# Moving one weight split, two activations and one later split in the start-up of a short-convolution kernel

## The chip, the cores and the metric

The kernel runs on one core of a Trainium2 chip. The core has five engines that run their own instruction queues in order and meet only through semaphores: TensorE (PE, matrix products; PEld is its weight load), VectorE (DVE, element-wise work), ScalarE (ACT, activations and copies), GpSimd (POOL, element-wise work on SBUF) and SyncE (SP, which issues the DMA transfers). Matrix products are written to PSUM, which has eight banks of 128 x 512 fp32 here; everything else lies in SBUF or in DRAM. The metric is the device time of one execution in microseconds; lower is better. A comparison of this kernel can tell two versions apart when they differ by about 0.2% of the time.

## The reference, cut to what matters

The depth is one, so that only the gated short-convolution layer runs, on 1024 tokens of width 1024, with an inner width of 2048:

```python
def short_conv_mixer(u, w_in, conv_w, w_out):
    z, bg, cg, v = jnp.split(u @ w_in.astype(u.dtype), 4, axis=-1)
    y = bg * causal_dwconv(cg * v, conv_w) * jax.nn.silu(z)
    return y @ w_out.astype(u.dtype)

u = rms_norm(h, pre_norm[i])
m = short_conv_mixer(u, sc_w_in[j], sc_conv_w[j], sc_w_out[j])
h = h + rms_norm(m, post_norm[i])
```

## The kernel before, in words

The result has to have fp32 accuracy. Each fp32 operand is therefore split into an upper part (a rounded copy, made by ScalarE) and a lower part (operand minus copy, made by VectorE), and a product of two operands becomes three matmuls: lower by upper, upper by lower, upper by upper (lines 189 to 191). `split` (lines 139 to 141) does this for a weight; `split_w(p, part)` names the tiles `w`.

The first multiplication, by `w_in`, takes the 64 column blocks of 128 two at a time: 32 pairs, two for each of 16 chunks of the inner width. Pair 2c holds the columns `cg` and `v` of chunk c, pair 2c+1 holds `z` and `bg`. Each pair is a 2 x 2 block product done with seven products instead of eight (Strassen's scheme in Winograd's form). The products are called a, b, c, e, d, f, g and run in this order on TensorE; each has 12 matmuls of 128 x 128 by 128 x 512. Products a, c, d and g add up in one PSUM bank, x; e and f in a second, v; b has a third, y. Before a next product may add to a bank, what stands in it has to be read: `snap` copies the bank behind products a, c and e to a tile `sna`, `snc` or `sne` (ScalarE, line 197), and a VectorE addition reads the bank behind b, d and f (lines 213, 218, 223). So d waits for the copy behind c, f for the copy behind e, and g for the addition `sne` behind d.

The weights of a pair are needed in four parts. Part 0 and part 3 are splits of raw blocks: part 0 is A11 and A12 (products a and b), part 3 is A22 (product g). Parts 1 and 2 are splits of four sums S that GpSimd forms in `add_s` (lines 133 to 137): part 1 serves c and e, part 2 serves d and f. On the other side stand the blocks `u` of the normalised, transposed input: `u_a`, `u_b`, `u_e`, `u_f` are parts of it, and `u_c`, `u_d`, `u_g` are split from differences T (lines 537 to 543, `t_sub`); `u_g` comes from -T4, which the second `t_sub` call writes. All `u` stay in SBUF through the whole first half.

The order on each engine is the program's order, written out by hand; no scheduler moves anything. Up to line 568 stands the head: pair 0 is multiplied in the plain way (no Strassen) while the input is normalised and transposed (`turn2`, `second`), with the products of pair 1 between, which end with c, e, d, f, g at lines 549 to 563. Behind the head comes a loop over the pairs 2 to 31; in pair 2 the function `first_chunk` adds to each product the work that completes chunk 0 (its convolution `cv`, two Silu activations, multiplications, and the store `y_d`). In each pair the loop also splits the weights of the next pair: part 0 behind b, part 1 behind e, part 2 behind f and part 3 behind g. `fetch` queues the load of a pair's raw weights on SP; three buffers, `raw`, take turns, and one of their turns is taken by the split `w1_1`.

The second half multiplies by `w_out` in the same manner from line 691 on.

In the text below, `w3_1` is part 3 of pair 1 (tile numbers of a profile row are left out there: it reads `w<-raw`), `w0_2` is part 0 of pair 2, and so on. An upper copy of a weight is the ACT row `L140`, a lower part the DVE row `L141`.

Of the kernel before, what the change touches and what calls it, by code (L numbers as in the profile page):

```python
# [8 lines left out]
F32 = mybir.dt.float32  # L9
# [9 lines left out]
def kernel(  # L19
# [16 lines left out]
    nc = tc.nc  # L36
# [32 lines left out]
    def flat(t):  # L69
        return t.rearrange("p a b -> p (a b)")  # L70
# [52 lines left out]
    def add_s(p, part):  # L123

        if p >= len(PAIRS):
            return
        r = raws[p]
        a11, a12, a21, a22 = (flat(r[:, n, k * KH : (k + 1) * KH]) for n in (0, 1) for k in (0, 1))
        if part == 0:
            sums[p] = raw.tile([P, 4, HB], F32, tag="sum", name=f"sum_{p}", bufs=1)  # L130
        s = sums[p]
        if part == 0:
            nc.gpsimd.tensor_add(s[:, 1], a21, a22)  # L133
            nc.gpsimd.tensor_sub(s[:, 0], s[:, 1], a11)
        else:
            nc.gpsimd.tensor_sub(s[:, 2], a11, a21)  # L136
            nc.gpsimd.tensor_sub(s[:, 3], a12, s[:, 0])  # L137

    def split(src, hi, lo):
        nc.scalar.copy(hi, src)  # L140
        nc.vector.tensor_sub(lo, src, hi.bitcast(F32))  # L141

    def split_w(p, part):

        if p >= len(PAIRS):
            return
        n = 2 * HB if part < 3 else HB
        tag = "w8" if part < 3 else "w4"
        if p == 1 and part == 1:
            t = raw.tile([P, 2, n], F32R, tag="raw", name=f"w{part}_{p}")  # L150
        else:
            t = wp.tile([P, 2, n], F32R, tag=tag, name=f"w{part}_{p}", bufs=3 if part < 3 else 2)
        if part == 0:
            src = flat(raws[p][:, 0])
        elif part == 3:
            src = flat(raws[p][:, 1, KH:])
        else:
            src = flat(sums[p][:, 2 * (part - 1) : 2 * part])
        split(src, t[:, 0], t[:, 1])
        wt[p, part] = t  # L160
# [4 lines left out]
    UH, UL = {}, {}  # L165
# [10 lines left out]
    def product(p, i, ks=None):  # L176

        part, off = WHERE[i]
        w = wt[p, part]
        which = {"b": "y", "e": "v", "f": "v"}.get(i, "x")  # L180
        first = i in "abe"
        if first and (p, which) not in banks:
            banks[p, which] = bank(f"p{which}_{p}")
        ps = banks[p, which]
        for k in range(KH) if ks is None else ks:
            hi = w[:, 0, off + k * P : off + (k + 1) * P]
            lo = w[:, 1, off + k * P : off + (k + 1) * P]
            last = k == KH - 1
            nc.tensor.matmul(ps, lo, UH[i][:, k], start=first and k == 0, stop=False, skip_group_check=True)  # L189
            nc.tensor.matmul(ps, hi, UL[i][:, k], start=False, stop=False, skip_group_check=True)  # L190
            nc.tensor.matmul(ps, hi, UH[i][:, k], start=False, stop=last, skip_group_check=True)  # L191
# [12 lines left out]
    def after(p, i):  # L204


        c = p // 2
        x_, v_ = banks[p, "x"], banks.get((p, "v"))
        if i in "ace":
            snap(p, i)  # L210
        if i == "b":
            t = sn[p, "a"]
            nc.vector.tensor_add(t, banks[p, "y"], t)
        elif i == "c" and p % 2:
            nc.scalar.activation(sn[p, "a"], sn[p, "a"], AF.Silu)
        elif i == "d":
            t = sn[p, "e"]
            nc.vector.tensor_add(t, x_, t)  # L218
            if p % 2:
                nc.gpsimd.tensor_mul(t, t, cvs[c][:, HB:])  # L220
        elif i == "f":
            t = sn[p, "c"]
            nc.vector.tensor_add(t, v_, t)  # L223
            if p % 2:
                nc.scalar.activation(t, t, AF.Silu)
                nc.gpsimd.tensor_mul(cvs[c][:, HB:], t, sn[p, "e"])
            else:
                nc.gpsimd.tensor_mul(gpad[:, TAPS - 1 + HB :], t, sn[p, "e"])  # L228
        elif i == "g":
            if p % 2:  # L230
                cv = cvs[c][:, :HB]
                nc.vector.tensor_mul(cv, x_, cv)
                nc.vector.tensor_mul(cv, cv, sn[p, "a"])
                y_done(c, cvs.pop(c))
            else:
                nc.vector.tensor_mul(gpad[:, TAPS - 1 : TAPS - 1 + HB], x_, sn[p, "a"])
                conv(c)
# [4 lines left out]
    def y_done(c, cv):  # L242
        nc.sync.dma_start(y_d[:, c], cv)
        done[c] = cv
# [48 lines left out]
    bt = flat(xa).rearrange("p (q k l) -> p q k l", q=2, k=KH)  # L293
# [193 lines left out]
    def plain_late(kk, part):  # L487

        for n in (0, 1):
            plain(0, n, 1, part, [kk], first=part == 1 and kk == 0, last=part == 0 and kk == KH - 1)  # L490
# [12 lines left out]
    turn2(2)  # L503
    second(2)
    nc.vector.tensor_add(sn[1, "a"], banks[1, "x"], sn[1, "a"])
    split_w(1, 3)
    plain_late(0, 0)
    plain_late(1, 1)
    turn2(3)
# [11 lines left out]
    def halves(a, j):  # L521
        return a[:, 2 * j : 2 * j + 2].rearrange("p k (t l) -> p k t l", t=TH)

    def t_halves(i, src):
        hi, lo = ((lambda j, u=u: halves(u[i], j)) for u in (UH, UL))
        return (
            lambda j: nc.scalar.copy(hi(j), src(j)),
            lambda j: nc.vector.tensor_sub(lo(j), src(j), hi(j).bitcast(F32)),
        )

    def t_split(i, src):
        hi, lo = t_halves(i, src)
        for j in range(2):
            hi(j)
            lo(j)

    def t_sub(q):
        for j in range(2):
# [14 lines left out]
    product(1, "e")  # L553
    snap(1, "e")
    product(1, "d")
    g_hi, g_lo = t_halves("g", lambda j: halves(bt[:, 1], j))
    g_hi(0)
    g_lo(0)
    g_hi(1)
    nc.vector.tensor_add(sn[1, "e"], banks[1, "x"], sn[1, "e"])  # L560
    g_lo(1)
    product(1, "f")
    product(1, "g")
    split_w(2, 0)
# [12 lines left out]
    def conv(c):  # L577
        cv = tmp.tile([P, L], F32, tag="cv", name=f"cv_{c}", bufs=2)
        nc.scalar.activation(cv, gpad[:, :L], AF.Copy, scale=tap(c, 0))  # L579
        for j in range(1, TAPS):  # L580
            nc.vector.scalar_tensor_tensor(  # L581
                cv, gpad[:, j : j + L], tap(c, j), cv, op0=ALU.mult, op1=ALU.add
            )
        cvs[c] = cv

    def first_chunk(i):

        if i == "":
            g = gpad[:, TAPS - 1 : TAPS - 1 + HB]
            nc.scalar.copy(g, banks[0, 0, 0])  # L590
            nc.vector.tensor_mul(g, banks[0, 1, 0], g)
            nc.vector.tensor_mul(gpad[:, TAPS - 1 + HB :], sn[0, 0], sn[0, 1])
            split_w(2, 1)
            conv(0)
            nc.gpsimd.tensor_mul(cvs[0][:, HB:], cvs[0][:, HB:], sn[1, "e"])
        elif i == "a":
            split_w(2, 2)
        elif i == "b":
            cv = cvs[0]
            nc.scalar.activation(sn[1, "c"], sn[1, "c"], AF.Silu)  # L600
            nc.scalar.activation(sn[1, "a"], sn[1, "a"], AF.Silu)
            nc.gpsimd.tensor_mul(cv[:, HB:], cv[:, HB:], sn[1, "c"])
            split_w(2, 3)
        elif i == "c":
            cv = cvs.pop(0)
            nc.vector.tensor_mul(cv[:, :HB], banks[1, "x"], cv[:, :HB])
            nc.vector.tensor_mul(cv[:, :HB], sn[1, "a"], cv[:, :HB])
            y_done(0, cv)
# [40 lines left out]
    for p in range(2, len(PAIRS)):  # L649
        q, prev = p + 1, p // 2 - 1  # L650
        for i in ORDER:
            product(p, i)
            after(p, i)
            if p == 2:
                first_chunk(i)
            if i == "a" and p < END:
                add_s(q, 0)
                if p in TODO:
                    fetch_t(TODO[p])
                if p % 2 == 0 and p > 2:  # L660
                    fetch_s(prev)
                if p + 2 <= END:
                    fetch(p + 2)
            if p == END - 1 and i in "cd":
                fetch_unit()
            if p == END:
                if i in "abcdg":
                    split_unit()
                    fetch_unit()
            elif i == "b":  # L670
                split_w(q, 0)
                add_s(q, 1)
                if p in TODO:
                    add_t(TODO[p], nc.gpsimd if p % 2 else nc.vector)
                if p == 3 or p % 2 == 0 and p > 2:
                    add_y(prev)
            elif i == "e":
                split_w(q, 1)
            elif i == "f":
                split_w(q, 2)  # L680
            elif i == "g":
                split_w(q, 3)
# [149 lines left out]
```

## Time and profile before

| What | Value |
|---|---|
| median of 3 runs | 795.43 us (795.42 to 795.58) |
| the profiled execution's own time | 795.87 us |
| its span, first to last instruction | 794.1 us |
| PE busy | 783.7 us (99% of the span), 3502 matmuls |
| DVE busy | 531.8 us (67%) |
| ACT busy | 308.7 us (39%) |
| POOL busy | 290.9 us (37%) |
| DMA | 114.38 MB, mean 144 GB/s |

A row of the timeline gives the start and the length in microseconds, the engine, the line, the operation and its tiles, and in brackets how long the engine had been idle and what ended this. The end of a matmul is modelled, so that neighbouring matmuls overlap in the rows: how fast they follow each other is read from their starts. Several equal instructions in a row are shown as one with a count.

### The profile page before, as it was taken

What the parts mean: (1) busy time and instruction counts of PE and PEld (TensorE: products, weight loads), DVE (VectorE), ACT (ScalarE), POOL (GpSimd) and SP (SyncE); (2) the same over time, 40 slices, a digit from 0 to 9 for tenths busy, and PEclk for the clock granted to TensorE, in tenths of its full rate; (3) what the DMA queues carried; (4) which work ended last, traced back from release to release, by engine and by line L of the source; (5) the groups of instructions that cost most, each with busy time, mean ns of one, the idle gap of its engine ahead of it and who ended that gap; (6) DMA issues with size and microseconds to landing.
All of it is one profiled execution on the core that took longest, in us unless ns stands there. A gap on an engine that the chain in (4) does not pass through costs nothing.

```text
span 794.1 us, 9047 instructions
## 1 busy us (share of the span) xinstructions
PE 783.7 (99%) x3502; PEld 648.9 (82%) x3502; DVE 531.8 (67%) x578; ACT 308.7 (39%) x424; POOL 290.9 (37%) x196
## 2 busy tenths in 40 slices
PE   8999999999999999999999999999999999999996
PEld 7877888888888888888888888888888888888885
DVE  5799676767676767676666666666666857633766
ACT  7555333342433333333333332323333637544441
POOL 1608634443444444447444444444344100000020
PEclk9999999999999999999999999999999999999998
DMA  9130351516170706165433324141515669455237
GB/s 321 53 106 6 89 198 54 199 53 211 42 245 8 252 25 227 44 209 174 130 96 103 114 86 145 54 146 53 163 38 178 233 215 418 181 205 212 106 109 262
DMA packets 94282, 114.38 MB, mean 144 GB/s; under 512 B 2920, under 2 KB 68512, under 8 KB 92192
## 3 DMA queue, kind: packets, MB, share of 16 engines
q1 hardware_dynamic: 94224, 113.81, 42.1%
q8 instruction: 27, 0.44, 0.2%
q14 instruction: 15, 0.12, 0.0%
q10 hardware_dynamic: 16, 0.00, 0.0%
HBM read 84.44 MB, written 29.36 MB: 143 GB/s over the span
## 4 chain that ended last, share of the span: by engine, by line
PE 90%; issue 4%; POOL 3%; DMA 1%; DVE 1%; ACT 0%; SPq 0%; DVEq 0%; POOLq 0%
PE px L189 13%; PE px L190 13%; PE px L191 13%; PE pv L189 7%; PE pv L190 7%; PE pv L191 7%; PE po_x L711 4%; PE po_x L712 4%; PE po_x L710 4%; PE py L189 3%; PE py L191 3%; PE py L190 3%; PE po_v L711 2%; PE po_v L712 2%; PE po_v L710 2%
## 5 line engine op out<-in xcount | busy, mean ns | idle before, releaser
L141 DVE TENSOR_TENSOR w<-sum,w 128x1024 fp32r<-128x1024 f32 x62 | 92.6, 1493 | 80.9 <-ACT w L140 80.9
L141 DVE TENSOR_TENSOR w<-raw,w 128x1024 fp32r<-128x1024 f32 (+1 forms) x62 | 98.3, 1587 | 6.0 <-ACT w L140 6.0
L140 ACT CAST w<-sum 128x1024 fp32r<-128x1024 f32 x62 | 65.0, 1049 | 65.7 <-issue 54.5
L581 DVE SCALAR_TENSOR_TENSOR cv<-gpad,cw,cv 128x1024 f32<-128x1024 f32 x32 | 64.4, 2012 | 19.7 <-ACT cv L579 19.1
L140 ACT CAST w<-raw 128x1024 fp32r<-128x1024 f32 (+1 forms) x62 | 51.5, 833 | 60.3 <-PE py L191 58.7
L228 POOL TENSOR_TENSOR gpad<-snc,sne 128x512 f32<-128x512 f32 x15 | 19.4, 1296 | 138.9 <-DVE snc L223 138.9
L136 POOL TENSOR_TENSOR sum<-raw 128x512 f32<-128x512 f32 x31 | 61.6, 1986 | 0.0
L220 POOL TENSOR_TENSOR sne<-sne,cv 128x512 f32<-128x512 f32 x15 | 20.5, 1367 | 102.1 <-DVE sne L218 86.9
L223 DVE TENSOR_TENSOR snc<-pv,snc 128x512 f32<-128x512 f32 x30 | 20.7, 691 | 52.4 <-PE pv L191 52.4
L750 POOL TENSOR_TENSOR acc<-acc,xr 128x512 f32<-128x512 f32 x4 | 6.9, 1722 | 133.3 <-DVE acc L749 133.3
L137 POOL TENSOR_TENSOR sum<-raw,sum 128x512 f32<-128x512 f32 x31 | 55.2, 1780 | 0.0
L133 POOL TENSOR_TENSOR sum<-raw 128x512 f32<-128x512 f32 x31 | 41.5, 1338 | 32.5 <-DVE w L141 32.5
L189 PE MATMUL px<-u_g,w 128*128 128x512 f32 x124 | 48.4, 391 | 1.4 <-DVE sne L218 0.7
L189 PE MATMUL px<-u_d,w 128*128 128x512 f32 x124 | 48.4, 390 | 0.3 <-ACT snc L197 0.3
L189 PE MATMUL py<-u_b,w 128*128 128x512 f32 x124 | 48.4, 391 | 0.0
L189 PE MATMUL px<-u_a,w 128*128 128x512 f32 x124 | 48.3, 390 | 0.0
L190 PE MATMUL px<-u_d,w 128*128 128x512 f32 x124 | 48.3, 389 | 0.0
L190 PE MATMUL px<-u_g,w 128*128 128x512 f32 x124 | 48.3, 389 | 0.0
L191 PE MATMUL py<-u_b,w 128*128 128x512 f32 x124 | 48.3, 389 | 0.0
L191 PE MATMUL px<-u_a,w 128*128 128x512 f32 x124 | 48.2, 389 | 0.0
L190 PE MATMUL py<-u_b,w 128*128 128x512 f32 x124 | 48.2, 389 | 0.0
L190 PE MATMUL px<-u_a,w 128*128 128x512 f32 x124 | 48.2, 389 | 0.0
(253 smaller groups left out, 2071.8 us busy)
## 6 DMA issues: line engine op xcount, KB each, us to landing
raw<-in_sc_w_in SPq DMA_DIRECT2D x64, 512.0 KB, 5.3
y_d<-cv SPq DMA_DIRECT2D x16, 512.0 KB, 3.2
t<-in_sc_w_out SPq DMA_DIRECT2D x8, 1024.0 KB, 6.0
t_d<-t SPq DMA_DIRECT2D x8, 1024.0 KB, 4.3
s_d<-s SPq DMA_DIRECT2D x8, 768.0 KB, 3.3
s<-y_d SPq DMA_DIRECT2D x8, 512.0 KB, 4.5
xr<-in_x SPq DMA_DIRECT2D x8, 512.0 KB, 4.6
out<-acc SPq DMA_DIRECT2D x12, 256.0 KB, 2.5
```

The costliest lines, as they stand in the source:

```text
L133: nc.gpsimd.tensor_add(s[:, 1], a21, a22)
L136: nc.gpsimd.tensor_sub(s[:, 2], a11, a21)
L137: nc.gpsimd.tensor_sub(s[:, 3], a12, s[:, 0])
L140: nc.scalar.copy(hi, src)
L141: nc.vector.tensor_sub(lo, src, hi.bitcast(F32))
L189: nc.tensor.matmul(ps, lo, UH[i][:, k], start=first and k == 0, stop=False, skip_group_check=True)
L190: nc.tensor.matmul(ps, hi, UL[i][:, k], start=False, stop=False, skip_group_check=True)
L191: nc.tensor.matmul(ps, hi, UH[i][:, k], start=False, stop=last, skip_group_check=True)
L581: nc.vector.scalar_tensor_tensor(cv, gpad[:, j : j + L], tap(c, j), cv, op0=ALU.mult, op1=ALU.add)
L710: nc.tensor.matmul(ps, lo, u[:, 0, k], start=first, stop=False, skip_group_check=True)
L711: nc.tensor.matmul(ps, hi, u[:, 1, k], start=False, stop=False, skip_group_check=True)
L712: nc.tensor.matmul(ps, hi, u[:, 0, k], start=False, stop=last, skip_group_check=True)
```

## The change

Three things move. No arithmetic is added or taken away.

- The split `w3_1` (A22 of pair 1) stood in the head between the third and the fourth block of `turn2` and `second`. It now stands behind product d of pair 1. The addition `sne` follows it, and both halves of the split of `u_g` follow that; before, the addition stood between the lower parts of the two halves. A helper that let the halves be taken apart is gone with it.
- In pair 2 the two Silu activations of chunk 0 and the GpSimd multiplication that uses one of them stood behind product b; they now stand behind product c. The multiplications of the first half of chunk 0 and its store stood behind c and now stand behind d.
- The split of part 1 of pair 3, in pair 2, stood behind product e and now stands behind product d. In all later pairs it stays behind e.

```diff
     nc.vector.tensor_add(sn[1, "a"], banks[1, "x"], sn[1, "a"])
-    split_w(1, 3)
     plain_late(0, 0)
...
     def t_split(i, src):
-        hi, lo = t_halves(i, src)
         for j in range(2):
-            hi(j)
-            lo(j)
+            hi, lo = (halves(u[i], j) for u in (UH, UL))
+            split(src(j), hi, lo)
...
     product(1, "d")
-    g_hi, g_lo = t_halves("g", lambda j: halves(bt[:, 1], j))
-    g_hi(0)
-    g_lo(0)
-    g_hi(1)
+    split_w(1, 3)
     nc.vector.tensor_add(sn[1, "e"], banks[1, "x"], sn[1, "e"])
-    g_lo(1)
+    t_split("g", lambda j: halves(bt[:, 1], j))
     product(1, "f")
...
         elif i == "b":
+            split_w(2, 3)
+        elif i == "c":
             cv = cvs[0]
             nc.scalar.activation(sn[1, "c"], sn[1, "c"], AF.Silu)
             nc.scalar.activation(sn[1, "a"], sn[1, "a"], AF.Silu)
             nc.gpsimd.tensor_mul(cv[:, HB:], cv[:, HB:], sn[1, "c"])
-            split_w(2, 3)
-        elif i == "c":
+        elif i == "d":
             cv = cvs.pop(0)
             nc.vector.tensor_mul(cv[:, :HB], banks[1, "x"], cv[:, :HB])
...
-            elif i == "e":
+            elif i == ("e" if p > 2 else "d"):
                 split_w(q, 1)
```

More of the change, by code (lines that the diff above doesn't have):

```diff
@@ L522, in halves @@
         return a[:, 2 * j : 2 * j + 2].rearrange("p k (t l) -> p k t l", t=TH)
[L524 to L529, printed above, removed]
     def t_split(i, src):
-        hi, lo = t_halves(i, src)
         for j in range(2):
-            hi(j)
-            lo(j)
+            hi, lo = (halves(u[i], j) for u in (UH, UL))
+            split(src(j), hi, lo)
     def t_sub(q):
```

## The prediction

> **What bounds the kernel now.** I read the page's busy times first, then TensorE's view of waits, then its timeline around each wait, then the timelines of the engines that ended them.
>
> ```profile
> PE 783.7 (99%) x3502; PEld 648.9 (82%) x3502; DVE 531.8 (67%) x578; ACT 308.7 (39%) x424; POOL 290.9 (37%) x196
> ```
>
> TensorE is busy for 783.7 of 794.1 us. Another engine can matter only where TensorE stands still. Three of its waits lie in the stretch that the change touches:
>
> ```profile
> PE px L189 <- DVE sne L218: 0.7, 1, 0.7
> ...
> PE px L189 <- ACT w L140: 0.6, 1, 0.6
> ...
> PE px L189 <- ACT snc L197: 0.3, 1, 0.3
> ```
>
> In TensorE's timeline these are the starts of products g of pair 1, d of pair 2 and g of pair 2. The rows are the last matmul ahead of the first stop, the stopped ones, and the first matmuls of the products that serve as marks (12 matmuls each):
>
> ```profile
> 58.37 0.39 PE L191 MATMUL pv<-u_f,w 128*128 128x512 f32 x1
> 59.40 0.47 PE L189 MATMUL px<-u_g,w 128*128 128x512 f32 x1 [0.64 <-ACT w L140]
> 62.22 0.39 PE L189 MATMUL px<-u_a,w 128*128 128x512 f32 x1
> ...
> 70.38 0.39 PE L189 MATMUL pv<-u_e,w 128*128 128x512 f32 x1
> ...
> 73.55 0.50 PE L189 MATMUL px<-u_d,w 128*128 128x512 f32 x1 [0.29 <-ACT snc L197]
> ...
> 76.45 0.39 PE L189 MATMUL pv<-u_f,w 128*128 128x512 f32 x1
> ...
> 80.05 0.50 PE L189 MATMUL px<-u_g,w 128*128 128x512 f32 x1 [0.72 <-DVE sne L218]
> ...
> 82.90 0.39 PE L189 MATMUL px<-u_a,w 128*128 128x512 f32 x1
> ```
>
> From 62.22 to 70.38 three products (a, b, c) pass without a stop: 8.16 us, 2.72 each, 0.227 per matmul. With that pace each stop is priced by starts, which also takes in the slow first matmul behind it (0.47 to 0.50 long):
>
> - g of pair 1: it could start at 58.37 + 0.227 = 58.60 and a at 61.32; a starts at 62.22. Lost: 0.90.
> - d of pair 2: from e at 70.38, f could start at 75.82; it starts at 76.45. Lost: 0.63.
> - g of pair 2: from f at 76.45, a of pair 3 could start at 81.89; it starts at 82.90. Lost: 1.01.
>
> Together 2.54 us. TensorE's view of waits names none behind 82.90, so time gained here stays gained unless a new stop arises.
>
> **The change, part by part.**
>
> *First part: w3_1 and sne.* VectorE in the head:
>
> ```profile
> 40.95 1.17 DVE L141 TENSOR_TENSOR w<-raw,w 128x512 fp32r<-128x512 f32 x1
> 42.04 0.74 DVE L480 SCALAR_TENSOR_TENSOR xb<-pk,gcol,xa 128x512 f32<-128x512 f32 x1
> ...
> 53.90 2.35 DVE L543 TENSOR_TENSOR xa<-xa,xb 128x1024 f32<-128x1024 f32 x2
> 57.43 1.23 DVE L528 TENSOR_TENSOR u_g<-xa,u_g 128x1024 fp32r<-128x1024 f32 x1 [1.18 <-ACT u_g L527]
> 58.57 0.68 DVE L560 TENSOR_TENSOR sne<-px,sne 128x512 f32<-128x512 f32 x1
> 59.17 1.21 DVE L528 TENSOR_TENSOR u_g<-xa,u_g 128x1024 fp32r<-128x1024 f32 x1
> 60.30 1.22 DVE L141 TENSOR_TENSOR w<-raw,w 128x1024 fp32r<-128x1024 f32 x1
> ```
>
> Product g (59.40) starts just behind the end of the addition `sne` (58.57 + 0.68 = 59.25), although the page's row names the copy of another weight. The addition stood behind the first lower half of `u_g`, and that behind a gap of 1.18. Product d had ended long before: its last matmul is 12 places ahead of 58.37, at 55.65, and 0.39 long, so at 56.04. ScalarE in the same stretch, and the transposes that the earlier VectorE row has to wait for:
>
> ```profile
> 40.03 1.03 PE L347 MATMUL pk<-ident,xb 128*128 128x128 f32 x8
> ```
> ```profile
> 53.35 0.59 ACT L197 COPY sne<-pv 128x512 f32<-128x512 f32 x1 [1.21 <-PE pv L191]
> 56.34 2.01 ACT L527 CAST u_g<-xa 128x1024 fp32r<-128x1024 f32 x2 [2.40 <-DVE xa L543]
> 58.24 1.04 ACT L140 CAST w<-raw 128x1024 fp32r<-128x1024 f32 x1
> ```
>
> Taking w3_1's lower part out frees 42.04 - 40.95 = 1.09 us of VectorE. The next row needs the transposes, which end at 41.06, so VectorE runs 0.98 ahead from there, and `t_sub` ends at 55.27 instead of 56.25. Its upper part goes into ScalarE's 2.40 gap ahead of `u_g`, and costs nothing there. Its lower part comes behind `t_sub`: 0.68 to 1.17 us. The 1.17 is the row above, taken while GpSimd worked; the 0.68 is the 128x512 addition. I take 0.68, since GpSimd has nothing to do at that place before the head is over: 55.95. Then `sne`, not before 56.04: done by 56.8. The new wait of VectorE on d therefore costs some 0.1; behind it stand both halves of `u_g` and w0_2. First half of `u_g`: its copy (56.34 - 0.98 = 55.36, about 1.0 long) is there at 56.4, so it ends at 58.0; the second at 59.2; w0_2's lower part at 60.4. TensorE asks for them at 58.83 (second matmul of g), 60.19 (its eighth) and 61.32 (a). Slack 0.8, 1.0 and 0.9: the stop goes, **-0.90**. With no head start at all and with 1.17, `sne` ends at 58.1, the first half at 59.3, and g is held 0.5: the gain is then 0.4.
>
> The load of pair 3 now takes the buffer of `w1_1`, free when e ends (53.32), and not that of w3_1's block at 42.1; pair 4's takes the latter, behind 55.95. Both stand on SP's queue with nothing urgent between.
>
> ```profile
> raw<-in_sc_w_in SPq DMA_DIRECT2D x4, 512.0 KB, 5.0
> ```
>
> That is the DMA view of 30 to 70 us, the four loads of pairs 3 and 4: 5.0 us to landing, so pair 3 lies in SBUF near 59. It is first read at about 68 (below). Cost nothing.
>
> *What follows from it.* GpSimd's sums for pair 2 start when `u_g` is done (head memory):
>
> ```profile
> 60.50 2.17 POOL L133 TENSOR_TENSOR sum<-raw 128x512 f32<-128x512 f32 x1
> ...
> 65.71 2.29 POOL L137 TENSOR_TENSOR sum<-raw,sum 128x512 f32<-128x512 f32 x1
> ```
> ```profile
> 65.18 1.67 DVE L141 TENSOR_TENSOR w<-sum,w 128x1024 fp32r<-128x1024 f32 x1 [0.57 <-ACT w L140]
> 66.77 3.63 DVE L581 SCALAR_TENSOR_TENSOR cv<-gpad,cw,cv 128x1024 f32<-128x1024 f32 x2
> 70.32 1.22 DVE L141 TENSOR_TENSOR w<-sum,w 128x1024 fp32r<-128x1024 f32 x1
> ```
>
> They move up by 60.38 - 59.2 = about 1.2, TensorE by 0.90. So w1_2 is whole at 66.85 - 1.2 = 65.65 and c of pair 2 asks at 61.32 + 5.44 = 66.76; w2_2 is whole at 70.3, d asks at 72.20. No stop.
>
> *Second part: Silu behind c.* ScalarE in pair 2:
>
> ```profile
> 68.03 1.06 ACT L140 CAST w<-sum 128x1024 fp32r<-128x1024 f32 x1 [1.37 <-POOL sum L137]
> 69.11 1.28 ACT L600 ACT_TABLE_LOAD   x1
> ...
> 71.47 1.56 ACT L140 CAST w<-raw 128x512 fp32r<-128x512 f32 x2
> 72.92 0.58 ACT L197 COPY snc<-px 128x512 f32<-128x512 f32 x1
> 73.40 0.58 ACT L197 COPY sne<-pv 128x512 f32<-128x512 f32 x1
> ```
>
> Table load and both Silus take 71.47 - 69.11 = 2.36, and `snc` stands behind them though c was over long before. After: the casts of w2_2 (66.8 to 67.9), w3_2 and w0_3 (to 69.4), then `snc` at c's end, 69.48 + 0.17 (the modelled 0.39 beyond the 0.227 step): 69.7 to 70.3. d asks at 72.20: **-0.63**. Load and Silus run from 70.2 to 72.6, and `sne` stands behind them: 72.6 to 73.2; f asks at 74.92, slack 1.7.
>
> The Trainium skill ("ScalarE: Activation LUTs", What ACT_TABLE_LOAD costs) counts about 1.38 us of drain beside 1.28 us for the load. Its load agrees with the row; of a drain the row shows nothing, since 2.36 - 1.28 leaves 1.08 for two Silus. By the page `sne` would end at 74.6, 0.3 ahead of f, and the sum would be the same.
>
> *Third part: splits of S, and the order on VectorE.*
>
> ```profile
> 72.10 3.36 DVE L141 TENSOR_TENSOR w<-raw,w 128x512 fp32r<-128x512 f32 x2
> ...
> 77.73 1.66 DVE L141 TENSOR_TENSOR w<-sum,w 128x1024 fp32r<-128x1024 f32 x1 [0.57 <-ACT w L140]
> 79.32 0.68 DVE L218 TENSOR_TENSOR sne<-px,sne 128x512 f32<-128x512 f32 x1
> ```
> ```profile
> 74.45 2.16 POOL L134 TENSOR_TENSOR sum<-sum,raw 128x512 f32<-128x512 f32 x1
> 76.57 1.74 POOL L602 TENSOR_TENSOR cv<-cv,snc 128x512 f32<-128x512 f32 x1
> ```
>
> Before, `sne` of pair 2 is behind w1_3, and w1_3 behind a sum of GpSimd's (74.45 + 2.16 = 76.61). After, `sne` comes first: VectorE has w3_2 and w0_3 done by 70.3 + 0.7 + 3.36 = 74.4, d ends at 75.1, `sne` at 75.8; g asks at 74.92 + 2.72 = 77.64, slack 1.8: **-1.01**. What is late next is w1_3, behind `sne` and chunk 0's two multiplications: near 79. It is asked for by c of pair 3, at 80.36 + 5.44 = 85.80. GpSimd's multiplication for chunk 0 (1.74) now follows the sums of pair 3; w2_3 gains by that, the store of chunk 0 and pair 5's load behind it on SP come about 2 us later, and pair 5 is read two pairs on. Cost nothing.
>
> **The sum.** -0.90 - 0.63 - 1.01 = -2.54 us. The profiled execution took 795.87 and would take 793.33. The median is 0.44 below it: 795.43 - 2.54 = **792.9 us**, 0.32% faster. About 0.2% (1.6 us) is what a measurement tells from no change.
>
> **The rivals.**
>
> - *The head gains half, or GpSimd is in the way.* Without head start and with the slow split g is held 0.5: 793.4. Nearly the same price has a collision: w1_2's lower part is ready to start at about 63.9, and if one of GpSimd's sums (up to 2.29) ran ahead of all of it, it would end at 63.9 + 2.29 + 1.22 = 67.4 and hold c 0.65: 793.5. For it speak the rows 1.67 against 1.22 of one form; against it, that they differ by 0.45, not by 2. Beside it the Trainium skill ("SBUF — State Buffer", Who interferes with whom) has the pair of ports that VectorE and GpSimd share as an exclusive lock for the whole instruction; by that rule 793.5 is the worst case.
> - *One stop comes back whole*, because another operation takes its place: the dearest gives 795.43 - 1.53 = 793.9.
> - *Nothing is gained*: VectorE stays the pace of the head and of pair 2, and TensorE waits later for what has been put off: 795.4. Against it: what is put off (w1_3) has 6 us of slack.
> - *Slower: pair 3's load.* It is issued 11 us later than before. ScalarE casts w0_3 ahead of `snc`, and d's slack is 1.9: landing behind about 70.1 holds TensorE one for one, and behind 72.7, 19 us after issue, the gain of 2.54 is used up; landing at 74 would give 796.7. Against it: 5.0 us to landing.
>
> **How the numbers follow.** All three stops gone: 0.74. First rival 0.10, second 0.06, third 0.05, slower 0.05. The predicted time is that of the first. The range goes from 792.4 (the 0.44 between profiled run and median, as play) to 793.9, the second rival; 0.10 of the cases lie above, and I keep 0.05 for play below. Faster by over 0.2% means below 793.84: 0.74 + 0.10 and half of 0.06, 0.87. Within: 0.08. Slower: 0.05.
>
> **What the profile would show.** Right: TensorE's three waits on L189 are gone, g of pair 1 starts near 58.6, a of pair 2 near 61.3, a of pair 3 near 80.4; the span is about 791.6. `sne` of pair 1 ends near 56.8, `snc` of pair 2 starts near 69.7. Wrong: a wait of g's second matmul on `u_g`, of c on w1_2 (GpSimd rows longer than 2 us in front of it), or of d on `snc` behind a late load; or a new wait behind 82.9.

## The result, and the profile after

| | before | after |
|---|---|---|
| median | 795.43 us (795.16 to 796.06) | 793.03 us (792.61 to 793.81) |
| profiled execution's span | 794.1 us | 790.8 us |
| PE busy | 783.7 us | 782.7 us |

The ratio of the times is 0.997, with a 95% interval of 0.9961 to 0.9979: 2.40 us or 0.30% faster. Forecast were 792.9 us, in a range of 792.4 to 793.9. As a gain the interval reads 1.7 to 3.1 us, so that a median 0.1 us from the forecast is in part luck; the distance worked out below is the sharper test.

The page's chain that ended last (followed back from the last instruction, at each step to what released it; `issue` is time in which nothing that the profile shows was waited for), of the kernel before, then the busy times and that chain of the changed kernel:

```profile
PE 90%; issue 4%; POOL 3%; DMA 1%; DVE 1%; ACT 0%; SPq 0%; DVEq 0%; POOLq 0%
```
```profile
PE 782.7 (99%) x3502; PEld 649.6 (82%) x3502; DVE 532.0 (67%) x578; ACT 308.6 (39%) x424; POOL 291.0 (37%) x196
...
PE 98%; DVE 0%; DMA 0%; ACT 0%; issue 0%; DVEq 0%
```

The work is the same to a microsecond. Nearly the whole chain is now TensorE's own, and GpSimd (3% before) is no longer in it. Its view of waits, complete:

```profile
PE pw L323 <- DVE idle L283: 1.1, 1, 1.1
PE pp L390 <- DVE u_a L360: 0.3, 1, 0.3
```

The three waits on L189 are gone, and no new one has come. The timeline of TensorE in the changed kernel, at the same marks as before (last matmul of f of pair 1, then g, a, e, d, f, g, a):

```profile
57.63 0.39 PE L191 MATMUL pv<-u_f,w 128*128 128x512 f32 x1
57.85 0.39 PE L189 MATMUL px<-u_g,w 128*128 128x512 f32 x1
...
60.57 0.39 PE L189 MATMUL px<-u_a,w 128*128 128x512 f32 x1
...
68.73 0.39 PE L189 MATMUL pv<-u_e,w 128*128 128x512 f32 x1
...
71.45 0.39 PE L189 MATMUL px<-u_d,w 128*128 128x512 f32 x1
...
74.17 0.39 PE L189 MATMUL pv<-u_f,w 128*128 128x512 f32 x1
...
76.89 0.39 PE L189 MATMUL px<-u_g,w 128*128 128x512 f32 x1
...
79.61 0.39 PE L189 MATMUL px<-u_a,w 128*128 128x512 f32 x1
```

Every product takes 2.72 us. From the last matmul of f of pair 1 to a of pair 3 it is 21.98 us, before 82.90 - 58.37 = 24.53: **2.55 us less, against 2.54 forecast.** This distance is the mark for all that follows. The two profiled spans differ by more, 3.3 us, because the mark itself starts at 57.63 instead of 58.37. That 0.74 lies ahead of the changed code: the last matmul of the plain multiplication with `u_b`, well ahead of the first thing that was moved (w3_1's lower part at 40.95), is 0.74 apart already (before, then after):

```profile
27.16 0.39 PE L391 MATMUL pp<-u_b,wn 128*128 128x512 f32 x1
```
```profile
26.42 0.39 PE L391 MATMUL pp<-u_b,wn 128*128 128x512 f32 x1
```
In the eleven profiles of this study the start lies anywhere from 57.63 to 58.37, and the profile before is the latest of them.

VectorE and ScalarE at the moved places of the changed kernel:

```profile
52.29 2.35 DVE L534 TENSOR_TENSOR xa<-xa,xb 128x1024 f32<-128x1024 f32 x2
54.56 0.68 DVE L141 TENSOR_TENSOR w<-raw,w 128x512 fp32r<-128x512 f32 x1
55.33 0.69 DVE L548 TENSOR_TENSOR sne<-px,sne 128x512 f32<-128x512 f32 x1
55.94 2.35 DVE L141 TENSOR_TENSOR u_g<-xa,u_g 128x1024 fp32r<-128x1024 f32 x2
58.21 1.22 DVE L141 TENSOR_TENSOR w<-raw,w 128x1024 fp32r<-128x1024 f32 x1
...
74.44 0.69 DVE L218 TENSOR_TENSOR sne<-px,sne 128x512 f32<-128x512 f32 x1 [1.07 <-PE px L191]
75.05 0.68 DVE L595 TENSOR_TENSOR cv<-px,cv 128x512 f32<-128x512 f32 x1
75.77 1.81 DVE L596 TENSOR_TENSOR cv<-sna,cv 128x512 f32<-128x512 f32 x1
77.50 2.32 DVE L141 TENSOR_TENSOR w<-sum,w 128x1024 fp32r<-128x1024 f32 x1
```
```profile
68.93 0.59 ACT L197 COPY snc<-px 128x512 f32<-128x512 f32 x1 [0.47 <-PE px L191]
69.54 1.28 ACT L590 ACT_TABLE_LOAD   x1
70.83 0.64 ACT L590 ACTIVATE snc<-snc 128x512 f32<-128x512 f32 x1
71.37 0.61 ACT L591 ACTIVATE sna<-sna 128x512 f32<-128x512 f32 x1
71.89 0.57 ACT L197 COPY sne<-pv 128x512 f32<-128x512 f32 x1
```

In pair 2 the addition `sne` and the copy `snc` now wait for TensorE ([1.07 <-PE], [0.47 <-PE]); before, TensorE waited for them. In pair 1 `sne` follows the split of w3_1 (54.56 + 0.68 = 55.24) after 0.1 us, the forecast wait for d.

### The profile page after: what moved, and what is told of

Its sections match the earlier page's. It is cut to its first block, busy times and chain, and to the rows that moved or that the text cites. A ratio compares the mean times of both kernels' runs of the same rounds, so it can differ in the third digit from the quotient of the medians.

```text
span 790.8 us, 9051 instructions
## 1 busy us (share of the span) xinstructions
PE 782.7 (99%) x3502; PEld 649.6 (82%) x3502; DVE 532.0 (67%) x578; ACT 308.6 (39%) x424; POOL 291.0 (37%) x196
## 4 chain that ended last, share of the span: by engine, by line
PE 98%; DVE 0%; DMA 0%; ACT 0%; issue 0%; DVEq 0%
PE px L191 14%; PE px L190 14%; PE px L189 14%; PE pv L191 7%; PE pv L189 7%; PE pv L190 7%; PE po_x L699 4%; PE po_x L700 4%; PE po_x L701 4%; PE py L189 4%; PE py L191 4%; PE py L190 4%; PE po_v L699 2%; PE po_v L700 2%; PE po_v L701 2%; PE pp L390 1%
## 5 line engine op out<-in xcount | busy, mean ns | idle before, releaser
L189 PE MATMUL py<-u_b,w 128*128 128x512 f32 x124 | 48.5, 391 | 0.0
L189 PE MATMUL px<-u_a,w 128*128 128x512 f32 x124 | 48.3, 390 | 0.0
L190 PE MATMUL px<-u_c,w 128*128 128x512 f32 x124 | 48.3, 389 | 0.0
L191 PE MATMUL px<-u_d,w 128*128 128x512 f32 x124 | 48.3, 389 | 0.0
L191 PE MATMUL px<-u_g,w 128*128 128x512 f32 x124 | 48.3, 389 | 0.0
L189 PE MATMUL px<-u_c,w 128*128 128x512 f32 x124 | 48.3, 389 | 0.0
```

## The experiments

What was open: whether the change removed three separate stops (theory 1), or whether the later two hang on the first through GpSimd's sums (theory 2); which half of the first part mattered; and how much room is left at the two places where something could have gone wrong. The two columns on the right are measured: the distance defined above, from one profile of each kernel, and the median.

| kernel | distance expected | distance | median, us |
|---|---|---|---|
| before | | 24.53 | 795.43 |
| first part only | 23.6 (theory 1), 23.2 (theory 2) | 23.24 | 794.02 |
| second part only | 23.9 (1), 24.5 (2) | 24.14 | 795.07 |
| third part only | 23.5 | 23.47 | 794.19 |
| second and third | 22.9 | 22.91 | 793.71 |
| only sne ahead of u_g | 23.9 | 23.94 | 794.90 |
| only w3_1 moved | 23.5 | 23.68 | 794.69 |
| all but the move of w3_1 | 22.0 | 22.04 | 792.86 |
| changed kernel | 22.0 | 21.98 | 793.03 |
| changed, six more copies | 23.3 | 24.21 | 795.08 |
| changed, late load of pair 3 | 24.7 | 23.99 | 795.36 |

Median less distance is 770.7 to 771.1 us in ten rows and 771.4 in the last. So what happens in these 25 us decides the time of each version, and nothing behind them gives it back. All medians of single parts lie within 1.6 us of the kernel before, and the intervals of the ratio given below reach 1 in three of them; what separates these versions is the distance, and the medians follow it.

**First part alone.** Edit, on the kernel before:

```diff
-    split_w(1, 3)
     plain_late(0, 0)
...
     product(1, "d")
+    split_w(1, 3)
     g_hi, g_lo = t_halves("g", lambda j: halves(bt[:, 1], j))
+    nc.vector.tensor_add(sn[1, "e"], banks[1, "x"], sn[1, "e"])
     g_hi(0)
     g_lo(0)
     g_hi(1)
-    nc.vector.tensor_add(sn[1, "e"], banks[1, "x"], sn[1, "e"])
     g_lo(1)
```

> Only the first part (w3_1 behind product d, sne behind it), pair 2 as before. The mark in all runs is the distance from the last matmul of product f of pair 1 to the first of product a of pair 3, which leaves out what happens while the input is loaded: 24.53 us before, 21.98 after. Theory 1, three separate stops: the stop of 0.90 goes and the two others stay, distance 23.6, time 794.5. Theory 2, a chain: the two later stops hang on GpSimd's sums, which start when u_g is done, 1.3 earlier here; sne of pair 2, and with it product g, comes 1.3 earlier, and d's stop vanishes beside it: distance 23.2, time 794.1.

Measured: distance 23.24, ratio 0.998 (0.9971 to 0.999). Theory 2. Of TensorE's waits on L189 one is left, at g of pair 2, and VectorE's row in front of it says why:

```profile
78.05 0.50 PE L189 MATMUL px<-u_g,w 128*128 128x512 f32 x1 [0.80 <-DVE sne L218]
```
```profile
75.72 1.67 DVE L141 TENSOR_TENSOR w<-sum,w 128x1024 fp32r<-128x1024 f32 x1 [0.57 <-ACT w L140]
77.31 0.68 DVE L218 TENSOR_TENSOR sne<-px,sne 128x512 f32<-128x512 f32 x1
```

`sne` still stands behind w1_3. The stop at d of pair 2 is gone without the second part, but for 0.12 us (d to f takes 2.84 instead of 2.72): the Silus come early enough once the sums do.

The chain that ended last in the profile before could have told this. From GpSimd's `gpad` memset at 60.45 it runs through GpSimd's sums, and on to g of pair 2 like this (start, length, engine, tile, line):

```profile
74.45 2.17 POOL sum L134
...
76.64 1.07 ACT w L140
...
77.73 1.66 DVE w L141
79.39 0.61 DVE sne L218
```

**The two halves of the first part.** Edits, each on the kernel before: only `sne` ahead of `g_hi(0)`; only `split_w(1, 3)` moved.

> Of the first part only the place of sne of pair 1: it stands ahead of both halves of u_g, w3_1 stays early, pair 2 as before. If the place of sne behind a half of u_g was what held product g: sne ends near 57, the first half of u_g near 58.7 (in the clock of the profile before), and g is not stopped; u_g is done 0.6 earlier, so GpSimd's sums are, and product g of pair 2 comes 0.6 earlier: distance 23.9, time 794.8. If VectorE's load by w3_1 was what held it, g of pair 1 stays stopped by 0.5 or more and the distance stays at 24.4.

> Of the first part only the move of w3_1; sne stays between the halves of u_g, pair 2 as before. If VectorE's load by w3_1 was what held product g: t_sub ends 1.0 earlier, sne near 58.2, ahead of g's 58.60, no stop; GpSimd's sums start 1.0 earlier, distance 23.5, time 794.4. If the place of sne alone counts, g of pair 1 stays stopped.

Measured: distances 23.94 and 23.68, ratios 0.9992 (0.9983 to 1.0002) and 0.999 (0.9981 to 1.0). In neither is g of pair 1 stopped; TensorE's waits on L189 are only those at d and g of pair 2. Each half alone thus removes the first stop. What differs is when GpSimd gets going, which is told by its memset of `gpad`. Before, first part, only `sne`, only w3_1, one row of each:

```profile
60.45 0.10 POOL L572 MEMSET gpad<- 128x2 f32 x1 [18.87 <-DVE u_g L528]
```
```profile
58.43 0.10 POOL L572 MEMSET gpad<- 128x2 f32 x1 [17.49 <-DVE u_g L527]
```
```profile
59.38 0.10 POOL L572 MEMSET gpad<- 128x2 f32 x1 [18.27 <-DVE u_g L528]
```
```profile
59.23 0.10 POOL L572 MEMSET gpad<- 128x2 f32 x1 [17.98 <-DVE u_g L527]
```

Counted from the last matmul of f (58.37, 57.70, 57.90, 58.03) it comes after 2.08, 0.73, 1.48 and 1.20 us: 1.35, 0.60 and 0.88 earlier than before. The distances are 1.29, 0.59 and 0.85 shorter. With pair 2 as it was, the gain is that of GpSimd's sums and not that of the stop in the head.

**Second part alone.** Edit, on the kernel before: the block with both Silus moves from behind b to behind c, the two multiplications and the store from behind c to behind d.

> Only the second part (Silu behind the copy of product c, chunk 0's first half behind d), head and splits of S as before. Theory 1: d's stop goes, 0.63, distance 23.9, time 794.8. Theory 2: d is no longer held, but sne of pair 2 still stands behind w1_3, which waits for GpSimd's sum ending near 76.6, so that product g starts at 80.05 as before and the time gained at d is lost again in a longer stop at g (1.5 instead of 1.0): distance 24.5, time 795.4, no gain at all.

Measured: distance 24.14, ratio 0.9994 (0.9984 to 1.0003), between the two expectations. TensorE's marks e, d, f, g of pair 2 and a of pair 3:

```profile
69.84 0.39 PE L189 MATMUL pv<-u_e,w 128*128 128x512 f32 x1
...
72.56 0.39 PE L189 MATMUL px<-u_d,w 128*128 128x512 f32 x1
...
75.28 0.39 PE L189 MATMUL pv<-u_f,w 128*128 128x512 f32 x1
...
79.06 0.50 PE L189 MATMUL px<-u_g,w 128*128 128x512 f32 x1 [0.90 <-DVE sne L218]
...
81.92 0.39 PE L189 MATMUL px<-u_a,w 128*128 128x512 f32 x1
```

The stop at d is gone, 0.63. From f to a it is 6.64 instead of 6.45, so the stop at g has grown from 1.01 to 1.20. Part of the gain is lost again, as theory 2 has it, but less than it wanted. The rest is a matter of w1_3's lower part:

```profile
77.18 1.23 DVE L141 TENSOR_TENSOR w<-sum,w 128x1024 fp32r<-128x1024 f32 x1 [2.27 <-ACT w L140]
```
```profile
76.03 1.30 POOL L136 TENSOR_TENSOR sum<-raw 128x512 f32<-128x512 f32 x1
77.29 2.25 POOL L137 TENSOR_TENSOR sum<-raw,sum 128x512 f32<-128x512 f32 x1
```

It took 1.23 us instead of 1.66: here VectorE was first by 0.11 and GpSimd's next sum was stretched to 2.25. In the kernel before, GpSimd's multiplication (76.57, 1.74 long) was already running when w1_3 began at 77.73, and VectorE's row was stretched. That the 0.43 gained comes from this order is read from the rows; no run here changes the order alone.

**Third part alone, and second and third together.** Edits, on the kernel before: the split of part 1 of pair 3 behind d; the same together with the second part.

> Only the third part (the split of w1_3 behind product d), head and Silu as before. Both theories: the stops of 0.90 and of 0.63 stay, g's goes: distance 23.5, time 794.4. If it were chunk 0's multiplications rather than w1_3 that hold sne of pair 2, g would still be stopped and the distance would stay over 24.

> Second and third part together, head as before. Both theories: 0.63 and 1.01 go, 0.90 stays: distance 22.9, time 793.8. Theory 1 wants this to be the sum of the runs with one part each; theory 2 wants more than their sum (nothing and 1.01). That all of the gain came from the head would leave 795.4.

Measured: distances 23.47 and 22.91, ratios 0.9984 (0.9975 to 0.9994) and 0.9977 (0.9967 to 0.9987). Both as expected. With the third part alone chunk 0's multiplications still stand ahead of `sne`, and g is not stopped: it was w1_3 that held it. Alone, the parts save 1.29, 0.39 and 1.06, which is 2.74 together; the change saves 2.55. The second and third together save 1.62, more than 0.39 + 1.06 = 1.45; the first adds 0.93 to them, but 1.29 when it is alone. So the stops are not separate. The last one, at g of pair 2, takes back what is gained ahead of it as long as `sne` hangs on GpSimd through w1_3.

**All but the move of w3_1.** Edit, on the kernel before: `sne` ahead of `g_hi(0)`, second and third part; `split_w(1, 3)` stays.

> All of the change but the move of w3_1: sne ahead of u_g, second and third part as in the changed kernel. If either half of the first part is enough for the first stop: no stop of TensorE on L189, distance 22.0, time 792.9. Its slacks are thin: u_g's first half ends 0.2 ahead of g's second matmul, w0_2 0.4 ahead of a. If the move of w3_1 is needed, g or a of pair 2 is held 0.2 to 0.5: distance 22.2 to 22.5.

Measured: distance 22.04, ratio 0.9967 (0.9954 to 0.998). No wait on L189. From g of pair 1 to a of pair 2 it is 2.78 instead of 2.72, which is all that the thin slacks cost:

```profile
58.05 0.39 PE L189 MATMUL px<-u_g,w 128*128 128x512 f32 x1
...
60.83 0.39 PE L189 MATMUL px<-u_a,w 128*128 128x512 f32 x1
```

The move of w3_1 is not needed for the gain; between this version and the changed kernel (792.86 and 793.03) the runs show no difference.

**Six more copies.** Edit, on the changed kernel:

```diff
             split_w(2, 3)
+        elif i == "e":
+            for _ in range(6):
+                nc.scalar.copy(sn[2, "e"], banks[2, "v"])
         elif i == "c":
```

> The changed kernel with the copy sne of pair 2 made seven times instead of once, into the same tile: six more ScalarE copies of 128x512 behind the Silus, 0.49 us apart. Predicted slack of product f behind the Silus: 1.7. If it is right, the last copy ends near 75.4 in the clock of the changed kernel's profile, f starts 1.3 later than 74.17, and all behind it: distance 23.3, time 794.3. If ScalarE has more room there than the rows show (copies that do not hold f), distance 22.0, time 793.0. If the Silus in front of sne had no slack, the loss would be all of the 2.9.

Measured: distance 24.21, ratio 0.9999 (0.9989 to 1.0008). The loss is 2.23 us, not 1.3:

```profile
72.15 0.57 ACT L197 COPY sne<-pv 128x512 f32<-128x512 f32 x1
72.75 3.68 ACT L590 COPY sne<-pv 128x512 f32<-128x512 f32 x6
```
```profile
71.71 0.39 PE L189 MATMUL px<-u_d,w 128*128 128x512 f32 x1
...
76.48 0.50 PE L189 MATMUL pv<-u_f,w 128*128 128x512 f32 x1 [1.88 <-ACT sne L590]
```

The six copies take 3.68, 0.61 each and not 0.49. They write the same tile; that this is why they do not overlap fits the spacing, but no run shows it by itself. The slack was right: the first copy ends at 72.72, f asks 2.72 behind d's 71.71, at 74.43, 1.7 later. 3.7 of copies less 1.7 of slack is 2.0, and the restart makes up the rest.

**A late load of pair 3.** Edit, on the changed kernel:

```diff
-    fetch(3)
...
             split_w(2, 2)
+            last = small.tile([P, 1], F32, tag="last", name="last", bufs=1)
+            nc.scalar.copy(last, wt[1, 1][:, 0, :1].bitcast(F32))
+            nc.scalar.copy(last, raws[1][:, 0, 0, :1])
+            fetch(3)
```

> The changed kernel with the load of pair 3 issued some 13 us later: two copies of one column by ScalarE, behind w2_2's upper part of pair 2, read the two buffers that the loads of pairs 3 and 4 take, so that these loads wait for them. Issue near 67.0 in the clock of the changed kernel's profile, landing 5.4 later, 72.4. By the prediction's fourth rival, w0_3 is then cast until 73.4, snc copied until 74.0, and product d, which asks at 71.45, is held 2.6; f is held 0.1 more behind the Silus: distance 24.7, time 795.7, the whole gain used up. If the load has more slack than that, distance 22.0 and time 793.0.

Measured: distance 23.99, ratio 0.9999 (0.9989 to 1.0009). The loss is 2.01 instead of 2.7:

```profile
67.15 4.18 SPq L121 DMA_DIRECT2D raw<-in_sc_w_in  x4
```
```profile
71.59 1.04 ACT L140 CAST w<-raw 128x1024 fp32r<-128x1024 f32 x1 [3.71 <-DMA raw<-in_sc_w_in]
72.54 0.58 ACT L197 COPY snc<-px 128x512 f32<-128x512 f32 x1
```
```profile
73.17 0.50 PE L189 MATMUL px<-u_d,w 128*128 128x512 f32 x1 [1.49 <-ACT snc L197]
```

The mechanism is the forecast one: the cast waits for the load, `snc` for the cast, d for `snc`. The half of the pair that ScalarE casts was there 4.4 us behind the issue, 0.8 earlier than expected. The time is that of the kernel before.

## Why the prediction was right

- **Which stops, and their price.** Right, to 0.01 us in the sum. Once no stop is left the distance is eight products of 2.72 and one step of 0.227, 21.99, however the stops hang together, so that this agreement does not prove that they were separate. The marks forecast (g 58.6, a 61.3, a of pair 3 80.4) were met when 0.74 is added to the clock after; the span, forecast as 791.6, was 790.8 because of that 0.74. Pricing by starts, against the pace of undisturbed products, was what did it: the waits view alone names 0.7 + 0.6 + 0.3 = 1.6.
- **First part.** The head start was forecast as 0.98. From the last matmul of f, `t_sub` ended 2.12 ahead before (53.90 + 2.35 against 58.37) and 2.99 ahead after (52.29 + 2.35 against 57.63): 0.87. The forecast let VectorE go on as the transposes end; it goes on 0.12 later (40.43 against 39.28 + 1.03). The split took 0.68, the value chosen. `sne` ended at 56.02, 1.61 ahead of f's last matmul; forecast was 56.8, 1.57 ahead. That GpSimd's sums would come about 1.2 earlier was forecast, and 1.35 measured in the run with this part alone. What the prediction did not say is that with pair 2 as it was these sums, and not the stop in the head, set the gain (1.29 with the first part alone, where the stop was priced at 0.90), and that either half of the edit is enough for the stop.
- **Second part.** `snc` starts when c ends, load and both Silus take 71.89 - 69.54 = 2.35 (forecast 2.36), slack of f 1.7. Of the drain of 1.38 us that the Trainium skill states ("ScalarE: Activation LUTs", What ACT_TABLE_LOAD costs) the rows show nothing: the load starts 0.02 behind the end of `snc`, the first Silu 0.01 behind the end of the load.
- **Third part.** `sne` waits for d alone. Mis-sized is what is late next: w1_3 ends at 79.82, in the clock of the profile before 80.6 instead of near 79, since chunk 0's second multiplication took 1.81 and w1_3 2.32 beside GpSimd's work. c of pair 3 asks at 85.06, so it cost nothing.
- **The sum.** Step by step each part was priced by its own stop, which gives the right total only when all three go. As prices of single edits the first two would have been wrong: 0.90 and 0.63 against 1.29 and 0.39 measured. The third is near, 1.01 against 1.06.
- **The rivals.** None came. The feared collision with GpSimd did not: w1_2's lower part took 1.67 as before and ended at 64.75 (63.08 + 1.67), 1.26 ahead of c at 66.01. The late load, made to happen, has the mechanism described, and a little more room: d asks at 71.45, the copy takes 0.58 and the cast 0.95 ahead of it, so that a landing behind 69.9 in the clock of the changed kernel, 70.7 in that of the profile before, holds TensorE one for one (forecast 70.1; 71.59 - 69.9 = 1.7 of the 2.0 measured, the rest is f behind the Silus and the restarts). Had the load come that late in the changed kernel, the gain would have been gone, as the run shows.

## What to carry to other kernels

Price a stop of the bounding engine by the starts of its work against its undisturbed pace, not by the wait that the profile names. Before adding up the stops that an edit removes, ask what the operand behind the last of them hangs on: while that chain is unchanged, it takes back what is gained earlier, and an edit that starts the chain earlier may gain more than its own stop. An instruction that another engine waits for belongs ahead of those that have slack on its in-order queue, even when it arrives later, as long as what is put behind it keeps some slack (six copies there used it up).

## What the runs showed that was not expected

- ScalarE copies of 128x512 that write the same tile follow each other at 0.61 us. Two copies that need nothing of each other started 0.48 apart in the profile before (72.92 and 73.40).
- Where w1_3's lower part on VectorE and a row of GpSimd's overlapped, the later to start was the longer one: VectorE 1.23 and GpSimd 2.25 with VectorE first, VectorE 1.66 with GpSimd first and 0.58 of its row to go. This agrees with the Trainium skill ("SBUF — State Buffer", Who interferes with whom), by which the first to issue keeps the shared ports for its whole instruction. As read from the rows of the second part alone, it moved a stop by 0.4 us. An addition that reads PSUM did not do it: beside `sne` of pair 2 in the changed kernel (74.44) GpSimd's row, 0.04 behind it, took 1.30.
- The start of the kernel, ahead of all that was changed, differs by up to 0.74 us between profiles. Differences of single spans below that say nothing about an edit; the distance between two marks does.
